# Two causal convolutions moved behind other products, a softplus cut in two, and one subtraction given to another engine, in a hybrid decoder layer

## The chip, the core and the metric

The kernel runs on one core of a Trainium2 chip. A core has a matrix engine (PE, whose weight loads are shown apart as PEld) and three engines for elementwise work: VectorE (DVE), ScalarE (ACT) and GpSimd (POOL). SyncE (SP) issues the DMA transfers. Each engine works through its own instructions in the order in which they were written, and semaphores make one engine wait for another. The metric is the time of one execution on the device in microseconds; the kernel before took 1659.45 us (median of 3 runs).

## The reference

One decoder layer over 1040 positions (16 learned positions ahead of 1024 tokens), width 1024, float32. The stage that the change touches is the first: normalised rows times the columns of `w_in`, and what hangs directly on them.

```python
xn = rms_norm(h, mix_pre_g)
proj = xn @ w_in                       # z | x,B,C | dt | q | k | v
xbc = silu(causal_dwconv(xbc, conv_w, conv_b))   # 4 taps a channel, then x, B and C
dt = softplus(dt_raw + dt_bias)
A = -exp(a_log)                        # decays come from cumulative sums of dt * A
...                                    # SSD mixer, stick-breaking attention, w_out, gated FFN
```

A causal depthwise convolution with four taps is, for each channel (a partition) and all 1040 positions, one multiply-add with the bias and three more multiply-adds.

## The kernel before

**Precision.** Every matrix product is made of three: each operand is split into a high part (rounded, written by ACT as a copy) and a low part (the operand minus its high part, by POOL or DVE), and high x high, low x high and high x low are summed. So each block of weights costs ACT a copy and POOL or DVE a subtraction before PE can use it. Names that end in `hi`/`h` are high parts, `lo`/`l` low ones: `whi4z` and `wlo4z` are the two parts of one block of z's weights.

**Products in pairs.** Two blocks of 128 output columns are made together by a scheme of seven half-size products (class `Duo`, `product`, lines 260 to 321) in place of eight. The order in which they are issued is 1, 6, 5, 7, 2, 3, 4, for the first pair (`i == 0`) 1, 5, 2, 6, 7, 3, 4. Each is 24 matmuls of 260 columns into one of three PSUM accumulators, which the trace calls `dA`, `dX` and `dY` followed by the pair's name (`dXx`, `dXz`). Products 6, 7 and 4 go into X one after another: each adds to what is there, and between them DVE (line 320, `craw_x<-dXx,...`) adds the accumulator's present value into the pair's rows `craw`. So the first matmul of the next product into the same accumulator waits for that DVE sum. Products 5 and 3 share Y in the same way, 1 and 2 share A, which ACT copies out (line 317).

**The pairs.** x00 (first two blocks of x), z00, x02, z02, then B/C of the second group, and so on. Weights of the following pair are prepared while one is multiplied: `split_22` (lines 273 to 279: ACT line 277, POOL line 278) for the block `a22`, `sums` (POOL, lines 281 to 288) for four sums of weights, `split_3`, `split_1`, `split_4` (ACT line 181, POOL line 182). For pair z00 these are `ahz`/`alz`, `wrz`/`s24z`, `whi3z`/`wlo3z`, `whi1z`/`wlo1z`, `whi4z`/`wlo4z`. Low parts of the activations' own sums (`t2l`, `t3l`, `t4l`, line 255) are made by DVE.

**Work hung into slots.** B and C of the first group were projected before the pairs. Their four taps (`tap`, lines 502 to 509: DVE, one TENSOR_SCALAR at line 505 and three SCALAR_TENSOR_TENSOR at line 508), the SiLU (ACT, line 512) and for B the turning by PE into token order (`to_tokens`, tiles `tt_B_0` to `tt_B_2`, evacuated by ACT at lines 492 and 497 into `xtkB`) are hung behind the seven products: `slots[j]` is issued after the j-th product of a pair, slot 7 after the first of the next. The same lists hold the parts of dt (`dt_acts`, line 625): `loads` (`fold`), `turn_dt` (18 small matmuls into `tpd`, line 649), the softplus (`soft_a`, `soft_b`: an exponential by ACT, then a series on DVE with tiles of 128x144) and the decays (`pz`).

**Orders and buffers that matter here.** PE, DVE, ACT and POOL keep the written order; SP's transfers are ordered by a planner. `tt_B_0`, `tt_B_1`, `tt_B_2` and `tpd` are taken in this order from one pool of two PSUM buffers: `tpd` gets the buffer of `tt_B_1`, and so waits until ACT has emptied that one.

Of the kernel before, what the change touches and what calls it, by code (L numbers as in the profile page):

```python
# [9 lines left out]
F32 = mybir.dt.float32  # L10
# [3 lines left out]
ALU = mybir.AluOpType  # L14
# [52 lines left out]
def tile_layer(ctx: ExitStack, tc: tile.TileContext, x, meta, rows, parts,  # L67
               w_z, w_xbc, w_dt, w_q, w_k, w_v, w_out, w_up, w_down, out):
    nc = tc.nc
# [15 lines left out]
    def psum_mm(name):  # L85
        return ps[0].tile([P, 512], F32, tag="mm", name=name, bufs=ps[1])
# [86 lines left out]
    def weight_rows(flat, n, o):  # L173
        return flat[:, o:o + n * WR].rearrange("p (k c) -> p k c", c=WR)[:, :, :P]
# [77 lines left out]
    def split_t(raw, hl, eng):  # L252
        h, l = hl
        nc.scalar.activation(h, raw, AF.Copy)
        eng.tensor_tensor(l, raw, h.bitcast(F32), op=ALU.subtract)
        return hl

    class Duo:
# [11 lines left out]
        def split_1(self):  # L270
            self.w["a11"], self.w["a12"] = split_w(self.r[0], f"1{self.nm}")

        def split_22(self):
            h, l = (weight_rows(sa.tile([P, 5 * P], F32R, tag=f"a22{e}", name=f"a{e}{self.nm}", bufs=2), 4, OFF22)
                    for e in "hl")
            raw = self.r[1][:, HI4]
            nc.scalar.activation(h, raw, AF.Copy)
            nc.gpsimd.tensor_tensor(l, raw, h.bitcast(F32), op=ALU.subtract)
            self.w["a22"] = h, l

        def sums(self):
# [217 lines left out]
    def conv_acts(b, raw, nm, turned, store):  # L499
        box = {}  # L500

        def tap(j):
            if j == 0:
                box["d"] = sa.tile([P, L], F32, tag="cd", name=f"cd{nm}", bufs=2)
                nc.vector.tensor_scalar(box["d"], raw[:, 0:L], conv_w[:, b, 0:1], conv_b[:, b:b + 1],
                                        op0=ALU.mult, op1=ALU.add)
            else:
                nc.vector.scalar_tensor_tensor(box["d"], raw[:, j:j + L], conv_w[:, b, j:j + 1], box["d"],
                                               op0=ALU.mult, op1=ALU.add)

        def silu():
            nc.scalar.activation(box["d"], box["d"], AF.Silu)
            if store is not None:
                nc.sync.dma_start(out=store, in_=box["d"])

        def skip():
            xd = raw[:, 0:L]
            nc.scalar.activation(xd, box["d"], AF.Copy, scale=ssd_d[:, b:b + 1])
            nc.sync.dma_start(out=xdd[b // 4][b % 4], in_=xd)

        def turn_(part):
            if part == 0:
                box["t"] = s3.tile([P, NT + 1, P], F32, tag="xtk", name=f"xtk{nm}", bufs=2)
            to_tokens(box["d"], box["t"], nm, part)
            if part == 2:
                turned(box["t"])

        taps_ = [lambda j=j: tap(j) for j in range(4)] + [silu] + [skip] * (b < 8)
        return taps_, [lambda k=k: turn_(k) for k in range(3)] if turned else []
# [16 lines left out]
    def store_bn(g):  # L546
        def store(t):
            nc.sync.dma_start(out=bnd[g][:NM, 0], in_=t[:NM, 0])
            nc.sync.dma_start(out=bnd[g][:, 1:], in_=t[:, 1:])
        return store  # L550
# [58 lines left out]
    b0_taps, b0_turns = conv_acts(8, chains[0][0], "B0", store_bn(0), bcd[0][0])  # L609
# [15 lines left out]
    def dt_acts():  # L625
        box = {}

        def t3(name):
            return s3.tile([P, NT + 1, 16], F32, name=name, tag=name)
# [26 lines left out]
        def soft_a():  # L656
            dtx = box["dtx"]
            e, s, s2 = box["e"], box["s"], box["s2"] = [t3(n) for n in ("e1", "s1", "s2")]
            nc.vector.scalar_tensor_tensor(e, dtx, -1.0, dtx, op0=ALU.mult, op1=ALU.min)
            nc.scalar.activation(e, e, AF.Exp)  # L660
            nc.vector.tensor_scalar(s, e, 2.0, None, op0=ALU.add)
            nc.vector.reciprocal(s, s)
            nc.vector.tensor_tensor(s, s, e, op=ALU.mult)
            nc.vector.tensor_tensor(s2, s, s, op=ALU.mult)
# [13 lines left out]
        def decay(k):  # L678
            lhs = (tri, low, ones)[k]
            pz, adt, dst = psum_mm(f"pz{k}"), box["s2"], dtk[:, 2 + k]  # L680
            w0 = P if k == 2 else NM
            mm(pz[:w0, 0:16], lhs[:NM, :w0], adt[:NM, 0, :], start=True, stop=True)
            mm(pz[:, 16:NA], lhs, adt[:, 1:, :], start=True, stop=True)
            nc.scalar.activation(dst[:w0, 0, :], pz[:w0, 0:16], AF.Exp)
            nc.scalar.activation(dst[:, 1:, :], pz[:, 16:NA].rearrange("p (a b) -> p a b", b=16), AF.Exp)
            if k == 0:
                nc.vector.tensor_copy(dtk[:NM, 1, 0, :], pz[:NM, 0:16])
                nc.vector.tensor_copy(dtk[:, 1, 1:, :], pz[:, 16:NA].rearrange("p (a b) -> p a b", b=16))
# [15 lines left out]
        def store():  # L704
            nc.sync.dma_start(out=dtkd, in_=dtk)

        return [[loads], [turn_dt], [soft_a], [soft_b], [lambda: decay(0)], [lambda: decay(1)],
                [lambda: decay(2), store, turn_acs]]

    v_stack = ExitStack()  # L710
# [2 lines left out]
    def fetch_v(kh, fh, pool, name="q", key=None):  # L713
        tiles = []
        for s in range(2):
            if pool is None:
                tiles.append(wp.tile([P, 2, 512], F32, tag="wraw", name=f"v{name}{kh}{fh}{s}"))
            else:
                tiles.append(pool.tile([P, 2, 512], F32, tag=f"v{kh}{fh}{s}", name=f"v{name}{kh}{fh}{s}"))
            r0 = (4 * kh + 2 * s) * P  # L720
            nc.sync.dma_start(out=tiles[s], in_=w_v[r0:r0 + 2 * P, 512 * fh:512 * fh + 512].rearrange(
                "(b p) c -> p b c", p=P))
        vq[key or (kh, fh)] = tiles
# [9 lines left out]
    def v_split(n, s):  # L733
        raw = vq[VRAW[VSPEC[n][0]]][s]
        h, l = (wp.tile([P, 2, 512], F32R, tag=f"w{e}", name=f"vw{e}{n}{s}", bufs=WB) for e in ("hi", "lo"))
        nc.scalar.activation(h, raw, AF.Copy)
        nc.vector.tensor_tensor(l, raw, h.bitcast(F32), op=ALU.subtract)
        vops[n, s] = h, l

    def merged(*lists):  # L740
        return [sum(parts_, []) for parts_ in zip(*lists)]

    c0_taps, _ = conv_acts(10, chains[1][0], "C0", None, bcd[0][1])
    dts = dt_acts()
    slots = [b0_taps[:2] + dts[0], b0_taps[2:4], b0_taps[4:], [], c0_taps[:2] + b0_turns[:1],
             c0_taps[2:4] + b0_turns[1:2], c0_taps[4:] + b0_turns[2:], dts[1]]
    for i, q in enumerate(duos):
        n = duos[i + 1] if i + 1 < len(duos) else None
        if i + 2 < len(duos):
            duos[i + 2].load()  # L750
        for j, m in enumerate((1, 5, 2, 6, 7, 3, 4) if i == 0 else (1, 6, 5, 7, 2, 3, 4)):
            q.product(m)
            if i == 0:
                if m == 1:
                    d0.split_4()
                elif m == 6:
                    split_t(t4l.bitcast(F32), xo["t4"], nc.vector)
            if n is not None:
                if m == 1:
                    n.split_22()  # L760
                elif m == 6:
                    n.sums()
                elif m == 7:
                    n.split_3()
                elif m == 2:
                    n.split_1()
                elif m == 3:
                    n.split_4()
            elif m in (7, 2):
                v_split(1, int(m == 2))  # L770
            for act in slots[j]:
                act()
        extra = slots[7:]
        slots = q.done(q)
        for k, acts_ in enumerate(extra):
            slots[k] = acts_ + slots[k]
        if i == 1:
            slots = merged(slots, [[], dts[2], [], dts[3], [], [], []]) + [dts[4], dts[5], dts[6]]
        if i == n_early:
            t_stack.close()  # L780
            vl = v_stack.enter_context(tc.tile_pool(name="vl", bufs=1, side="left"))
            fetch_v(1, 0, vl)
        if i + 2 == len(duos):
            fetch_v(0, 0, None)
# [887 lines left out]
    op = opool.enter_context(tc.tile_pool(name="outp", bufs=2, side="right"))  # L1672
# [574 lines left out]
    for i in range(2, NFF):  # L2247
        q = probs[i]
        n = probs[i + 1] if i + 1 < NFF else None
# [73 lines left out]
    slots = [ta.tile([P, 4 * HW], F32, tag=f"{n}{e}", name=f"slot{n}{e}") for n in ("b22", "t4") for e in "hl"]  # L2323
# [48 lines left out]
    for s in range(n2):  # L2372
        n, a, b, p = steps2[s]
# [122 lines left out]
```

## Time and profile before

| what | us |
|---|---|
| median of 3 runs (1658.9 to 1659.69) | 1659.45 |
| the profiled execution | 1663.12 |
| its span, first to last instruction | 1661.4 |
| PE busy in it | 1627.9 |
| DVE, ACT, POOL busy | 1091.1, 747.7, 780.6 |

The stage of the first projections with its pairs runs from the span's start to about 330 us. In rows of a timeline the columns are start, duration, engine, line, operation, out<-in and shape, and in brackets the engine's idle time before it and what ended that. PE's matmuls overlap: 24 of them start 0.12 us apart, so that a product takes 2.88 us. Between 162 and 330 us PE is busy all the time; between 50 and 162 it has a few short waits, which the prediction shows.

### The profile page before, as it was taken

How to read it: one execution, taken by the hardware profiler on the slowest of the kernel's cores; microseconds unless marked ns; L12 is line 12 of the kernel's file. 1: busy time of each engine (PE TensorE's matmuls, PEld its weight loads, DVE VectorE, ACT ScalarE, POOL GpSimd, SP SyncE). 2: the span in 40 equal slices, each digit the busy share in tenths (PEclk: the TensorE clock that was granted, in tenths of full speed). 3: DMA queues.
4: the chain of work that ended last, by engine and by line, in shares of the span. 5: the costliest groups of instructions: out<-in, count | busy, mean ns of one | idle time of the engine just before them, and what ended most of it. 6: DMA issues, size and time to landing. Idle time of an engine off the chain costs nothing.

```text
span 1661.4 us, 28993 instructions
## 1 busy us (share of the span) xinstructions
PE 1627.9 (98%) x11508; PEld 1433.2 (86%) x11508; DVE 1091.1 (66%) x1248; ACT 747.7 (45%) x1100; POOL 780.6 (47%) x579
## 2 busy tenths in 40 slices
PE   7999999999999999999999999999999999999998
PEld 6999999978777788888877889999999999888886
DVE  7975744344367689999840677766566655658877
ACT  7444344332234367767652435433333333344544
POOL 2876877520357463455431113777777767200001
PEclk9999999999999999999999999999999999999999
DMA  4543235334577776545254542232233332495335
GB/s 175 184 152 132 102 120 195 134 136 146 144 223 237 248 224 198 153 142 152 68 178 148 176 165 90 96 96 95 95 98 109 114 106 83 140 331 175 95 116 182
DMA packets 164518, 247.39 MB, mean 149 GB/s; under 512 B 18487, under 2 KB 99495, under 8 KB 162702
## 3 DMA queue, kind: packets, MB, share of 16 engines
q1 hardware_dynamic: 163806, 244.48, 45.8%
q8 instruction: 91, 1.49, 0.4%
q10 hardware_dynamic: 576, 1.05, 0.2%
q14 instruction: 45, 0.37, 0.1%
HBM read 161.99 MB, written 83.46 MB: 148 GB/s over the span
## 4 chain that ended last, share of the span: by engine, by line
PE 86%; DVE 4%; DMA 3%; POOL 3%; issue 2%; SPq 1%; ACT 1%; POOLq 0%; DVEq 0%; ACTq 0%
PE fX L1900 10%; PE mo L1504 10%; PE dnA L2312 7%; PE fY L1900 7%; PE fA L1900 7%; PE dnB L2312 5%; PE av L1352 3%; PE tw L1332 3%; PE z L1308 3%; DVE kp L1314 2%; PE dXz L308 2%; PE dXqk L308 2%; PE vA L819 2%; PE pj_q L218 2%; PE pj_k L218 2%
## 5 line engine op out<-in xcount | busy, mean ns | idle before, releaser
L1314 DVE TENSOR_TENSOR_SCAN kp<-kp,hold 128x396 f32<-128x396 f32 (+5 forms) x224 | 211.1, 1013 | 20.2 <-ACT kp L1309 18.3
L182 POOL TENSOR_TENSOR wlo<-wr,whi 128x1024 fp32r<-128x1024 f32 x43 | 99.3, 2318 | 41.0 <-ACT whi L181 41.0
L2349 POOL TENSOR_TENSOR fms<-fms 128x1 f32<-128x1 f32 x8 | 2.3, 287 | 222.0 <-DMA ar<-fda 185.9
L181 ACT ACTIVATE whi<-wr 128x1024 fp32r<-128x1024 f32 x43 | 45.7, 1063 | 112.2 <-PE fX L1900 73.5
L1972 DVE SCALAR_TENSOR_TENSOR ga<-gr,pp,ga 128x1024 f32<-128x1024 f32 x44 | 69.3, 1575 | 34.0 <-ACT ga L1965 33.2
L2234 ACT ACTIVATE dh<-ar 128x512 fp32r<-128x512 f32 x77 | 48.6, 631 | 94.7 <-PE dnB L2312 44.7
L2235 DVE TENSOR_TENSOR dl<-ar,dh 128x512 fp32r<-128x512 f32 x77 | 53.2, 691 | 47.1 <-ACT dh L2234 47.1
L1309 ACT ACTIVATE kp<-z 128x788 f32<-128x788 f32 (+4 forms) x96 | 72.7, 832 | 16.6 <-PE z L1308 12.2
L1337 ACT ACTIVATE th<-tw 128x1024 f32<-128x1024 f32 (+2 forms) x96 | 70.8, 813 | 15.6 <-PE tw L1332 15.6
L1352 PE MATMUL av<-th,v 128*64 128x128 f32 x1152 | 70.0, 275 | 2.0 <-POOL tmsa L985 0.9
L1332 PE MATMUL tw<-ident,kp 128*128 128x128 f32 x576 | 70.0, 276 | 0.8 <-DVE kp L1314 0.4
L1352 PEld LDWEIGHTS av<-th,v 128*64 128x64 f32 x1152 | 62.3, 137 | 8.1 <-issue 3.9
L1332 PEld LDWEIGHTS tw<-ident,kp 128*128 128x128 f32 x576 | 62.4, 141 | 8.0 <-issue 7.0
L2312 PE MATMUL dnA<-dl,dh 128*128 128x512 f32 x176 | 68.5, 389 | 0.0
L2312 PE MATMUL dnA<-dh 128*128 128x512 f32 x176 | 68.5, 389 | 0.0
L2312 PE MATMUL dnA<-dh,dl 128*128 128x512 f32 x176 | 68.5, 389 | 0.0
L1286 POOL TENSOR_SCALAR cb<-kp 128x32 f32<-128x32 f32 x64 | 42.9, 678 | 50.6 <-DVE kp L1314 44.3
L2033 POOL TENSOR_TENSOR al<-wr,ah 128x512 fp32r<-128x512 f32 x20 | 28.6, 1431 | 77.5 <-ACT ah L2032 77.4
L1308 PE MATMUL z<-k,q 64*128 64x396 f32 (+9 forms) x672 | 62.3, 329 | 1.0 <-DVE st L941 1.0
L1308 PEld LDWEIGHTS z<-k,q 64*128 64x128 f32 x672 | 53.1, 185 | 10.7 <-ACT th L1337 4.2
L2312 PE MATMUL dnB<-dh 128*128 128x512 f32 x132 | 51.3, 389 | 0.0
L2312 PE MATMUL dnB<-dh,dl 128*128 128x512 f32 x132 | 51.3, 389 | 0.0
(987 smaller groups left out, 6027.2 us busy)
## 6 DMA issues: line engine op xcount, KB each, us to landing
wr<-in_w_up SPq DMA_DIRECT2D x44, 512.0 KB
fds<-ga SPq DMA_DIRECT2D x44, 256.0 KB
b<-in_w_down SPq DMA_DIRECT2D x44, 256.0 KB
ar<-fds SPq DMA_DIRECT2D x44, 256.0 KB
fda<-ga SPq DMA_DIRECT2D x33, 256.0 KB
ar<-fda SPq DMA_DIRECT2D x33, 256.0 KB
k<-qkd SPq DMA_DIRECT2D x8, 1040.0 KB
q<-qkd SPq DMA_DIRECT2D x64, 128.0 KB
```

What stands on the lines that cost most here:

```text
L182: nc.gpsimd.tensor_tensor(l, raw, h.bitcast(F32), op=ALU.subtract)
L218: mm(acc[:, :CQ - s], a[:, k, :], b[:, k % 4, c + s:c + CQ], start=(k == 0 and j == 0), stop=(k == KB - 1 and j == 2))
L1308: mm(z[:, j, a - lo:e - lo], u[h, :], r[h, a - bases[x]:e - bases[x]], start=s_ == 0, stop=s_ == 2)
L1309: nc.scalar.activation(kp[:, :, lo:top], z[:, :, :top - lo], AF.Sigmoid, scale=-QSCALE)
L1314: nc.vector.tensor_tensor_scan(part, part, hold[:, L - last + a:L - last + e][:, ::-1], 1.0 if e == last else kp[:, j, e:e + 1], op0=ALU.m ...
L1332: nc.tensor.transpose(tw[:, j, b, :], kp[:, j, c0:c0 + P], ident)
L1337: copied[0] = nc.scalar.activation(th[:, :, :nb, :], tw[:, :, :nb, :], AF.Copy, scale=-1.0, bias=1.0).ins
L1352: mm(av[halves[j], 1 - x, :], v[:, kb, halves[j]], th[:, j, b, :], start=kb == 0, stop=kb == i)
L1504: recent[0] = mm(acc, u[:, k, :], v[:, cs], start=(k == 0 and j == 0), stop=(k == 7 and j == 2))
L1900: mm(acc[:, c, :nn], u[:, k, :], v[:, k, c0:c0 + nn], start=first and k == 0 and j == 0, stop=k == 3 and j == 2, skip_group_check=not first)
L1972: nc.vector.scalar_tensor_tensor(v, self.g[jj][:, :, i:i + 256], fconv_w[:, j, i:i + 1], v, op0=ALU.mult, op1=ALU.add)
L2312: mm(banks[BANK[n], t], u[:, 0, c], v[:, 1, :], start=(n in (1, 2, 5) and p == 0 and i == 0), stop=(p == NPR - 1 and i == 2), skip_group_c ...
```

## The change

Three edits, all in the first stage. First, `slots` of pair x00: B's first two taps move from behind its first product to behind its second, B's other taps and C's taps follow one place later each or are regrouped, and the turning of B goes with them. Second, `soft_a` ends after the exponential; the four DVE instructions that followed it become `soft_m`, hung one product later. Third, the low part of z00's block `a22` (`alz`, line 278) is made by DVE in place of POOL; later pairs keep POOL.

```diff
-        def split_22(self):
+        def split_22(self, eng=nc.gpsimd):
...
             nc.scalar.activation(h, raw, AF.Copy)
-            nc.gpsimd.tensor_tensor(l, raw, h.bitcast(F32), op=ALU.subtract)
+            eng.tensor_tensor(l, raw, h.bitcast(F32), op=ALU.subtract)
...
             nc.vector.scalar_tensor_tensor(e, dtx, -1.0, dtx, op0=ALU.mult, op1=ALU.min)
             nc.scalar.activation(e, e, AF.Exp)
+
+        def soft_m():
+            e, s, s2 = box["e"], box["s"], box["s2"]
             nc.vector.tensor_scalar(s, e, 2.0, None, op0=ALU.add)
             nc.vector.reciprocal(s, s)
             nc.vector.tensor_tensor(s, s, e, op=ALU.mult)
...
-        return [[loads], [turn_dt], [soft_a], [soft_b], [lambda: decay(0)], [lambda: decay(1)],
+        return [[loads], [turn_dt], [soft_a], [soft_m], [soft_b], [lambda: decay(0)], [lambda: decay(1)],
                 [lambda: decay(2), store, turn_acs]]
...
-    slots = [b0_taps[:2] + dts[0], b0_taps[2:4], b0_taps[4:], [], c0_taps[:2] + b0_turns[:1],
-             c0_taps[2:4] + b0_turns[1:2], c0_taps[4:] + b0_turns[2:], dts[1]]
+    slots = [dts[0], b0_taps[:2], b0_taps[2:3], b0_taps[3:], c0_taps[:1], c0_taps[1:3] + b0_turns[:1],
+             c0_taps[3:] + b0_turns[1:2], b0_turns[2:] + dts[1]]
...
-                    n.split_22()
+                    n.split_22(nc.gpsimd if i else nc.vector)
...
-            slots = merged(slots, [[], dts[2], [], dts[3], [], [], []]) + [dts[4], dts[5], dts[6]]
+            slots = merged(slots, [[], dts[2], dts[3], [], dts[4], [], []]) + [dts[5], dts[6], dts[7]]
```

DVE during the first pair, from the low part of t3 (`t3l`) to the sum of product 6 (`craw_x_840<-dXx`), before:

```order
L505 TENSOR_SCALAR cdB_851<-craw_B_256,pp 128x1040
L508 SCALAR_TENSOR_TENSOR cdB_851<-craw_B_256,pp,cdB_851 128x1040
L636 TENSOR_TENSOR fold<-ident 32x16
L255 TENSOR_TENSOR t3l<-t3r,t3h 128x2080
L320 TENSOR_TENSOR craw_x_838<-dYx_867,craw_x_838 128x520
L508 SCALAR_TENSOR_TENSOR cdB_851<-craw_B_256,pp,cdB_851 128x1040 x2
L320 TENSOR_TENSOR craw_x_840<-dXx_926,craw_x_838 128x520
```

The same stretch of DVE, and on to the sum of product 7, with the change:

```order
L255 TENSOR_TENSOR t3l<-t3r,t3h 128x2080
L278 TENSOR_TENSOR alz_848<-wrz_802,ahz_847 128x4x128
L636 TENSOR_TENSOR fold<-ident 32x16
L320 TENSOR_TENSOR craw_x_838<-dYx_864,craw_x_838 128x520
L505 TENSOR_SCALAR cdB_890<-craw_B_256,pp 128x1040
L508 SCALAR_TENSOR_TENSOR cdB_890<-craw_B_256,pp,cdB_890 128x1040 x2
L320 TENSOR_TENSOR craw_x_840<-dXx_923,craw_x_838 128x520
L255 TENSOR_TENSOR t4l<-t4l,t4h 128x2080
L508 SCALAR_TENSOR_TENSOR cdB_890<-craw_B_256,pp,cdB_890 128x1040
L320 TENSOR_TENSOR craw_x_838<-dXx_923,craw_x_838 128x520
```

B's first two taps stood ahead of `t3l` and now stand between the sums of products 5 and 6, where `alz` was added too; one tap left that place for one behind `t4l`.

ACT at the end of the first pair: the evacuations of B's three turned tiles (`xtkB<-tt_B_0`, `_1`, `_2`) and the SiLU of C (`cdC<-cdC`), before:

```order
L492 ACTIVATE xtkB_991<-tt_B_0_992 16x128
L181 ACTIVATE whi4z_1020<-s24z_954 128x8x128
L497 ACTIVATE xtkB_991<-tt_B_1_1026 128x512
L512 ACTIVATE cdC_988<-cdC_988 128x1040
L497 ACTIVATE xtkB_991<-tt_B_2_1059 128x512
```

And with the change:

```order
L181 ACTIVATE whi4z_1015<-s24z_951 128x8x128
L492 ACTIVATE xtkB_1021<-tt_B_0_1022 16x128
L512 ACTIVATE cdC_988<-cdC_988 128x1040
L497 ACTIVATE xtkB_1021<-tt_B_1_1053 128x512
L317 ACTIVATE craw_z_1088<-dAz_1063 128x520
```

The evacuation of `tt_B_1` stood ahead of C's SiLU and now stands behind it. PE's own rows there keep their order (`tt_B_2`, then `tpd`, then product 6 of z00), only the turnings of B lie one product later among them.

DVE in the third pair, between the sums of products 6, 5 and 7 (tile `e` is the softplus's exponential, `s` what follows from it), before:

```order
L659 SCALAR_TENSOR_TENSOR e_1403<-dtx 128x144
L661 TENSOR_SCALAR s_1404<-e_1403 128x144
L662 RECIPROCAL s_1404<-s_1404 128x144
L663 TENSOR_TENSOR s_1404<-s_1404,e_1403 128x144
L664 TENSOR_TENSOR s_1405<-s_1404 128x144
L320 TENSOR_TENSOR craw_x_1349<-dYx_1412,craw_x_1349 128x520
```

And with the change:

```order
L659 SCALAR_TENSOR_TENSOR e_1403<-dtx 128x144
L320 TENSOR_TENSOR craw_x_1349<-dYx_1408,craw_x_1349 128x520
L664 TENSOR_SCALAR s_1404<-e_1403 128x144
L665 RECIPROCAL s_1404<-s_1404 128x144
L666 TENSOR_TENSOR s_1404<-s_1404,e_1403 128x144
L667 TENSOR_TENSOR s_1405<-s_1404 128x144
```

The sum of product 5 moved ahead of the four instructions on `s`.

## The prediction

> **What bounds the kernel now.** I read the page's busy times first, then the waits of PE in the stage that the change touches, then that stage in slices, then the chain of work, then the timelines of DVE, POOL and ACT.
>
> ```profile
> span 1661.4 us, 28993 instructions
> PE 1627.9 (98%) x11508; PEld 1433.2 (86%) x11508; DVE 1091.1 (66%) x1248; ACT 747.7 (45%) x1100; POOL 780.6 (47%) x579
> 162.00:330.00 168.00, 168.00 (x1406) 167.91 (x1405) 80.11 (x71) 64.97 (x87) 118.29 (x62) 1.00 0.40 141
> PE dYx L308 <- DVE craw_x L320: 1.3, 1, 1.3
> PE dXz L308 <- POOL wlo4z L182: 1.0, 1, 1.0
> PE dXx L308 <- DVE craw_x L320: 1.0, 1, 1.0
> PE dAx L308 <- ACT craw_x L317: 0.7, 1, 0.7
> PE dXx L308 <- POOL wlo4x L182: 0.3, 1, 0.3
> ```
>
> PE is the bound, and from 162 to 330 us it is busy without a break (168.00 of 168.00): what PE loses or gains before 162 arrives there whole. Between 50 and 165 us it waits five times (the five rows), 4.3 us in all. A second loss shows in the granted clock and in the chain:
>
> ```profile
> 67.75:71.16 3.41, 2.48 (x20) 2.49 (x21) 1.05 (x3) 2.90 (x2) 3.41 (x2) 1.00 0.82 318
> 81.40:84.81 3.41, 2.54 (x21) 2.26 (x20) 3.32 (x6) 1.90 (x3) 3.41 (x2) 1.00 0.49 167
> 84.82:88.22 3.40, 3.25 (x15) 3.25 (x16) 2.98 (x2) 0.66 (x2) 2.69 (x3) 0.50 0.78 312
> 84.97 4.35 PE dXz L308 x22
> 89.32 2.88 PE dYz L308 x24
> L649 PE MATMUL tpd<-fold,sq 32*128 32x16 f32 (+1 forms) x18 | 2.1, 250 | 0.0
> ```
>
> From 84.82 to 88.22 us the clock (third number from the end) is 0.50, and the product that runs then takes 4.35 us where the next takes 2.88: 1.47 us lost behind a wait of 1.0. The slice ahead held that wait and the 18 small matmuls of `tpd`, and lost the clock; the slice from 67.75, with a wait of 0.96, kept it.
>
> **How DVE and POOL share.** These rows carry the sum:
>
> ```profile
> 58.24 0.81 DVE L505 TENSOR_SCALAR cdB<-craw_B,pp 128x1040 f32<-128x1040 f32 x1
> 59.09 1.30 DVE L508 SCALAR_TENSOR_TENSOR cdB<-craw_B,pp,cdB 128x1040 f32<-128x1040 f32 x1
> 60.30 0.15 DVE L636 TENSOR_TENSOR fold<-ident 32x16 f32<-32x16 f32 x1
> 60.39 2.31 DVE L255 TENSOR_TENSOR t3l<-t3r,t3h 128x2080 fp32r<-128x2080 f32 x1
> 62.62 0.68 DVE L320 TENSOR_TENSOR craw_x<-dYx,craw_x 128x520 f32<-128x520 f32 x1
> 63.23 2.62 DVE L508 SCALAR_TENSOR_TENSOR cdB<-craw_B,pp,cdB 128x1040 f32<-128x1040 f32 x1
> 65.89 2.12 DVE L508 SCALAR_TENSOR_TENSOR cdB<-craw_B,pp,cdB 128x1040 f32<-128x1040 f32 x1
> 67.93 0.69 DVE L320 TENSOR_TENSOR craw_x<-dXx,craw_x 128x520 f32<-128x520 f32 x1
> 62.09 2.67 POOL L182 TENSOR_TENSOR wlo4x<-s24x,whi4x 128x1024 fp32r<-128x1024 f32 x1 [5.96 <-ACT whi4x L181]
> 64.71 2.20 POOL L278 TENSOR_TENSOR alz<-wrz,ahz 128x512 fp32r<-128x512 f32 x1
> 67.52 2.55 POOL L182 TENSOR_TENSOR wlo1z<-wrz,whi1z 128x1024 fp32r<-128x1024 f32 x1
> 68.67 0.39 PE L308 MATMUL dXx<-t3h,whi3x 128*128 128x260 f32 x1 [0.96 <-DVE craw_x L320]
> ```
>
> A tap takes 1.30 alone (59.09) but 2.62 at 63.23: POOL's `wlo4x` runs until 64.76, and the tap ends 1.09 after that. POOL's `alz` then ends at 66.91, 1.06 after the tap's end at 65.85; the next tap ends 1.10 after `alz`. The two take turns, whole instructions at a time; the one that waited pays 0.2 less than its free time. The sums out of PSUM (line 320) keep their 0.68 beside a running POOL. A half-size instruction of POOL costs 1.06 in its turn, a full one 2.06 (`wlo1z`: ends 70.07, the tap before it 68.01).
>
> **The change, part one: what stands ahead of product 6's sum.** PE's product 7 waits for DVE's sum at 67.93 (last row above). Before, DVE had done B's first two taps in the hole between `t2l` and `t3l`, while ACT made `t3h`. That hole stays, empty: `t3h` waits for `t2l` as it did.
>
> ```profile
> 58.35 1.95 ACT L254 ACTIVATE t3h<-t3r 128x2080 fp32r<-128x2080 f32 x1 [3.37 <-DVE t2l L255]
> 64.79 1.05 ACT L181 ACTIVATE whi1z<-wrz 128x1024 fp32r<-128x1024 f32 x1
> 48.29 0.68 DVE L407 TENSOR_TENSOR t4r<-t4r,t2r 128x512 f32<-128x512 f32 x1
> ```
>
> `t3l` ends at 62.70 as before. `alz` on DVE, free price 0.68 as for `t4r` of the same 512 elements, waits its turn behind `wlo4x` (64.76): 65.23. `fold` and the sum of product 5 (0.15, 0.68, each starting 0.08 before the last ends): 65.92. B's first tap starts at 65.84, 0.08 before POOL can start `wlo1z` (`whi1z` ends 65.84, and POOL started 0.08 after ACT at 62.09): 66.65. `wlo1z` 68.71, second tap 69.80, POOL's first sum of weights 70.86, third tap 71.95, sum of product 6 72.56. PE starts product 7 at 72.6 in place of 68.67: **+3.9**. If `wlo1z` wins the near tie, the first tap waits for it: 1.1 more. Without any turn of POOL after `wlo4x` the same list ends near 69.7 (+1.1); so the bounds are +1.1 and +5.0, and I take 3.9, since all rows above show turns.
>
> PE then idles from 67.7 to 72.6, through the whole slice 67.75 to 71.16. If that halves the clock in the next slice (to 74.57), PE loses half of 2.0 us: **+1.0**, bounds 0 and 1.7 (half a slice).
>
> **Part two: the second wait.**
>
> ```profile
> 81.41 0.18 PE L649 MATMUL tpd<-fold,sq 32*16 32x16 f32 x1
> 79.62 0.58 ACT L497 ACTIVATE xtkB<-tt_B 128x512 f32<-128x512 f32 x1
> 82.91 1.07 ACT L512 ACTIVATE cdC<-cdC 128x1040 f32<-128x1040 f32 x1 [2.71 <-DVE cdC L508]
> 118.33 2.19 POOL L182 TENSOR_TENSOR wlo3z<-wrz,whi3z 128x1024 fp32r<-128x1024 f32 x1
> ```
>
> From 68.67 to `tpd` at 81.41 PE needed 12.7 us without a wait; the same work stands there now, so PE reaches `tpd` at 72.6 + 12.7 + 1.0 = 86.3. But `tpd` takes the PSUM buffer of `tt_B_1`, whose evacuation (before at 79.62, ahead of the SiLU at 82.91) now stands behind C's SiLU on ACT. The SiLU needs C's fourth tap, so DVE's turns decide. From 71.95, with the prices above: POOL's second sum of weights 73.0; `t4l` (2.31 less 0.2) 75.1; third sum 76.2; B's fourth tap 77.3; fourth sum 78.3; C's first tap 78.9. ACT does B's SiLU and `whi3z` (1.07, 1.05) by 79.45, then `wlo3z` (2.19 alone, the row at 118.33) 81.7; C's second tap 82.8; `wlo4z` 84.9; third tap 86.0; sum of product 4 86.6; fourth tap, alone, 87.8; SiLU 88.95; evacuation 89.45. PE waits from 86.3 to 89.5: **+3.2**. `tpd` takes its 2.0, and product 6 of z00 starts at 91.5. Its slice (88.23 to 91.64) holds a wait and `tpd`, as the one from 81.40 did, so I take 0.50 until 95.05: 3.4 us at half clock lose 1.7, and the product ends at 91.5 + 2.9 + 1.7 = 96.1. Before, it ended at 89.32. **Difference +6.8**, in which the old wait for `wlo4z` and its 1.47 are already gone (`wlo4z` is ready by 84.9, under the new wait).
>
> [...]
>
> **Part three: the softplus.**
>
> ```profile
> 118.50 2.18 DVE L664 TENSOR_TENSOR s<-s 128x144 f32<-128x144 f32 x1
> 120.60 0.69 DVE L320 TENSOR_TENSOR craw_x<-dYx,craw_x 128x520 f32<-128x520 f32 x1
> 78.64 0.33 SPq L268 DMA_DIRECT2D wrz<-in_w_z  x1
> ```
>
> `s<-s` waits its turn behind the `wlo3z` of 118.33, and the sum of product 5, behind it on DVE, keeps product 3 waiting 1.3. With the sum ahead of those four that wait goes: **-1.3**. What is late instead is the sum of product 7, which product 4 needs one product (2.9 us) later: nothing. Splitting costs no instruction; giving `alz` to DVE takes 1.2 off POOL, which has slack in either case. SP issues the same transfers; z02's first weights now stand ahead of B's store, and the load still waits for the fourth sum of weights (78.64 before, 78.3 now).
>
> **The sum.** 6.8 - 1.3 = +5.5 us on the profiled execution (span 1661.4, whole 1663.12). That lies 3.7 above the median of the runs; I carry the difference over: 1659.45 + 5.5 = **1665.0**. Its own range: no half clocks (-2.7), or tie lost and a longer half clock (+1.1 and +1.7): 1662.3 to 1667.8.
>
> **Rivals.** (a) *The waits go and none comes*: DVE reaches product 6's sum in time, since its list there is only some 4.5 us long without POOL's turns. Then 1.03 + 1.47 + 1.3 = 3.8 are saved: 1655.7. Against it: every pair of overlapping rows shows turns, and the hole before `t3l` is wasted. 12%. (b) *Only the first wait comes*: if DVE and ACT gain 3 us before C's SiLU, `tpd` runs at 86.3 and z00's product 6 ends at 86.3 + 2.0 + 2.9 = 91.2, 1.9 after 89.32; less 1.3, that is +0.6: 1660.1. For it: the list behind 72.6 is long and each price small. Against it: most of it is POOL's own work, which nothing shortens. 14%. (c) *`tpd` at half clock*: its 18 matmuls take 2.0 more, with the tie lost as well: 1668.1. 4%. My forecast: 70%.
>
> **Numbers.** A measurement of this kernel tells 0.2%, 3.3 us, from no change. The forecast is slower by more in nearly all of its range (67 of 70), with (c) 71%; (b) and the forecast's lower end make 16% for within; (a), and the lucky end of (b), 13% for faster. The range 1658.3 to 1668.5 leaves out (a) and the tails.
>
> **What would show it.** Right: PE's wait for `craw_x` L320 before product 7 of about 5 us; a new wait of `tpd` for ACT `xtkB`, 2 to 4 us; no wait of `dXz` for `wlo4z` and none of product 3 of x02; slices at 0.50 after one or both. Wrong: product 7 still starting near 68.7, DVE instructions of 1.30 beside a busy POOL, or a `tpd` that does not wait.

## The result, and the profile after

The changed kernel takes 1669.28 us (median of 6 runs, 1668.04 to 1670.66) beside 1659.72 for the kernel before (6 runs, 1658.9 to 1662.85). The ratio is 1.0053, with a 95% interval of 1.0042 to 1.0064: 7.0 to 10.6 us slower. The prediction had the sign right and said 1665.0, with 1668.5 as the upper end of its range; the time lies 4.3 above the one and 0.8 above the other.

The profiled execution took 1668.39 us. Its page, and the waits of PE from 40 to 175 us (total, times, longest):

```profile
span 1666.7 us, 28993 instructions
PE 1631.9 (98%) x11508; PEld 1438.5 (86%) x11508; DVE 1087.6 (65%) x1249; ACT 748.1 (45%) x1100; POOL 775.0 (47%) x578
```

```profile
PE dXx L308 <- DVE craw_x L320: 5.0, 1, 5.0
PE tpd L649 <- ACT xtkB L497: 2.3, 1, 2.3
PE dAx L308 <- ACT craw_x L317: 0.6, 1, 0.6
PE dXx L308 <- POOL wlo4x L182: 0.3, 1, 0.3
```

The wait of product 7 for DVE's sum has grown from 1.0 to 5.0 us, and `tpd` waits for ACT's `xtkB`. The wait for `wlo4z` (1.0) and that of product 3 of x02 (1.3) are gone. The first products started 0.98 us earlier in this execution (first matmul into `dAx` at 53.56, before at 54.54), so 0.98 is added to a time of this timeline before it is compared with one of before. The rows that decide, from the timelines of DVE, POOL, ACT and PE:

```profile
64.87 0.80 DVE L505 TENSOR_SCALAR cdB<-craw_B,pp 128x1040 f32<-128x1040 f32 x1
65.70 5.33 DVE L508 SCALAR_TENSOR_TENSOR cdB<-craw_B,pp,cdB 128x1040 f32<-128x1040 f32 x2
70.96 0.69 DVE L320 TENSOR_TENSOR craw_x<-dXx,craw_x 128x520 f32<-128x520 f32 x1
...
64.93 2.80 POOL L182 TENSOR_TENSOR wlo1z<-wrz,whi1z 128x1024 fp32r<-128x1024 f32 x1 [0.59 <-ACT whi1z L181]
67.68 2.27 POOL L285 TENSOR_TENSOR wrz<-wrz 128x512 f32<-128x512 f32 x1
...
87.04 1.07 ACT L512 ACTIVATE cdC<-cdC 128x1040 f32<-128x1040 f32 x1 [6.24 <-DVE dtx L651]
88.02 0.58 ACT L497 ACTIVATE xtkB<-tt_B 128x512 f32<-128x512 f32 x1
...
71.70 0.58 PE L308 MATMUL dXx<-t3h,whi3x 128*128 128x260 f32 x1 [5.04 <-DVE craw_x L320]
...
88.65 0.42 PE L649 MATMUL tpd<-fold,sq 32*16 32x16 f32 x3 [2.31 <-ACT xtkB L497]
...
91.63 0.59 PE L308 MATMUL dXz<-t2h,whi4z 128*128 128x260 f32 x1
```

B's two further taps take 5.33 us together instead of 2.6 (twice the 1.30 of a tap alone, before), since `wlo1z` (2.80) and a sum of weights (2.27) get their turns between them. C's SiLU comes at 87.04, and only behind it is the buffer for `tpd` emptied. The same stretch by slices (PE busy, PEld, DVE, ACT, POOL, then the granted clock):

```profile
65.66:69.07 3.41, 1.00 (x9) 0.79 (x7) 3.34 (x3) 2.52 (x2) 3.41 (x2) 1.00 0.98 378
69.07:72.48 3.41, 0.78 (x3) 0.78 (x4) 3.41 (x3) 0.70 (x1) 3.33 (x3) 0.50 0.02 9
72.49:75.90 3.41, 3.41 (x18) 3.41 (x17) 3.41 (x2) 0.00 (x0) 3.33 (x2) 0.50 0.00 0
...
86.14:89.55 3.41, 1.10 (x11) 0.87 (x9) 0.89 (x2) 2.51 (x5) 0.00 (x0) 1.00 0.18 74
89.55:92.96 3.41, 3.41 (x17) 3.37 (x17) 1.18 (x4) 0.54 (x2) 3.12 (x3) 0.50 0.58 236
92.97:96.38 3.41, 3.41 (x18) 3.41 (x18) 2.10 (x1) 0.00 (x0) 3.33 (x3) 0.50 0.00 0
```

Behind each wait the clock is 0.50 for two slices, not for one. Product 7 takes 4.86 us (71.70 to 76.56), `tpd` 2.98, product 6 of z00 5.11 (to 96.74).

### The profile page after: what moved, and what is told of

Read it like the earlier page. It is cut to its first block, busy times and chain, and to the rows that moved or that the text cites. A ratio compares the mean times of both kernels' runs of the same rounds, so it can differ in the third digit from the quotient of the medians.

```text
span 1666.7 us, 28993 instructions
## 1 busy us (share of the span) xinstructions
PE 1631.9 (98%) x11508; PEld 1438.5 (86%) x11508; DVE 1087.6 (65%) x1249; ACT 748.1 (45%) x1100; POOL 775.0 (47%) x578
## 3 DMA queue, kind: packets, MB, share of 16 engines
q8 instruction: 91, 1.49, 0.4%
## 4 chain that ended last, share of the span: by engine, by line
PE 87%; DVE 3%; issue 2%; DMA 1%; SPq 1%; POOL 1%; ACT 0%; DVEq 0%; POOLq 0%; ACTq 0%
PE fX L1903 10%; PE mo L1507 10%; PE dnA L2315 7%; PE fY L1903 7%; PE fA L1903 7%; PE dnB L2315 5%; PE av L1355 4%; PE tw L1335 3%; PE z L1311 3%; PE dXz L308 2%; PE dXqk L308 2%; PE pj_q L218 2%; PE pj_k L218 2%; DVE kp L1317 2%; PE vB L822 2%
```

## The experiments

Theory 1 is the prediction's: the longer list ahead of product 6's sum, worked off in turns with POOL; then `xtkB` behind C's SiLU; and a half clock after each wait. The rivals: one edit alone does all of it (`alz` on DVE); the second wait is hidden anyway; half clocks are what costs, or they cost nothing. A further question is the base: the sum was made against one execution, 3.7 us above the median.

All runs are put on one scale here, since the later stages scatter from execution to execution (from the fourth pair to the end the profiles need 1507.2 to 1513.6 us, in no order that follows the edits). The kernels b_again, a_again and e1_soft to e9_both were measured on one chip, e10_tpd2 to e12_warm on a second and e13_late on a third, each beside the kernel before; between these groups only the ratios are compared. The columns are the time of each kernel's profile from the first matmul of product 1 of x00 to the first matmul of product 7 of x00, of `tpd`, of product 5 of z00 (where product 6 ends), and of product 1 of the fourth pair; and the median of the timed runs with its ratio to the kernel before, measured beside it.

| kernel | product 7 | tpd | product 5 of z00 | fourth pair | median us | ratio, 95% interval |
|---|---|---|---|---|---|---|
| before, first profile | 14.14 | 26.88 | 34.62 | 95.82 | 1659.72 | |
| before, second (b_again) | 14.12 | 26.83 | 34.54 | 94.19 | 1661.85 | 0.9999, 0.9990 to 1.0007 |
| changed, first profile | 18.14 | 35.08 | 43.17 | 102.82 | 1669.28 | 1.0053, 1.0042 to 1.0064 |
| changed, second (a_again) | 18.14 | 35.06 | 41.58 | 101.23 | 1669.22 | 1.0051, 1.0037 to 1.0064 |
| e1_soft | 14.15 | 26.87 | 35.37 | 95.55 | 1661.06 | 0.9997, 0.9987 to 1.0008 |
| e2_slots | 17.34 | 34.99 | 43.09 | 102.73 | 1669.88 | 1.0053, 1.0040 to 1.0065 |
| e3_alz | 20.51 | 34.66 | 41.18 | 100.83 | 1667.85 | 1.0041, 1.0028 to 1.0055 |
| e4_turn | 18.14 | 33.33 | 38.33 | 97.98 | 1665.20 | 1.0022, 1.0013 to 1.0032 |
| e7_hole | 13.94 | 32.16 | 40.28 | 99.95 | 1665.59 | 1.0032, 1.0020 to 1.0044 |
| e9_both | 13.95 | 28.31 | 33.31 | 92.95 | 1660.83 | 0.9996, 0.9987 to 1.0005 |
| e10_tpd2 | 13.95 | 28.31 | 36.67 | 96.50 | 1664.40 | 1.0015, 1.0006 to 1.0024 |
| e11_split | 13.95 | 28.29 | 33.49 | 96.11 | 1661.08 | 0.9998, 0.9989 to 1.0007 |
| e12_warm | 18.20 | 31.10 | 37.62 | 97.26 | 1662.10 | 1.0010, 1.0001 to 1.0019 |
| e13_late | 13.93 | 27.93 | 32.93 | 96.39 | 1662.28 | 1.0004, 0.9995 to 1.0013 |

### Both kernels again

> The kernel before, unchanged, profiled again. The profiled execution of before that the sum stood on took 1663.12 us, 3.7 above the median of its runs. If that execution was an ordinary one, this one shows the same waits and half clocks of PE (slices at 0.50 from 84.8 and from 470.5 us) and a span near 1661.4. If it was a slow one, the span is near 1658 and some of its waits or half-clock slices are gone: then the sum was made against the wrong base. In either case the ratio to the kernel before is 1.000.

> The changed kernel, unchanged, profiled and timed again beside the kernel before. If the loss is what its first profile shows against the second profile of before (8.6 us from the first product of the pairs to the first of the fourth pair), the ratio is 1.0045 to 1.006. If the forecast's base was sound and its sum right, 1.0025 to 1.0035. The profile shows the wait of product 7 of x00 near 5.0 us, that of tpd 2 to 3 us, and slices at 0.50 behind both.

Measured beside the kernel before again, the change gives 1.0051; the loss is real and not a matter of the first six runs. Its profile shows the two waits, 5.0 us for product 7 and 1.8 for `tpd`, a little under the 2 to 3 expected. The medians of the kernel before in the later comparisons, 15 to 27 runs each, are 1661.1 to 1661.7, about 2 us above the 1659.45 that the prediction started from. The second profile of before has a span of 1660.1 us, between the two that were expected, and the slice at 0.50 from 470.5 us isn't in it. Its waits of PE from 40 to 175 us:

```profile
PE dXz L308 <- POOL wlo4z L182: 1.0, 1, 1.0
PE dXx L308 <- DVE craw_x L320: 1.0, 1, 1.0
...
```

The wait of 1.3 us for the sum of product 5 ahead of product 3 of x02, which the prediction saved with the softplus, isn't there. From product 5 of z00 to the fourth pair this profile needs 59.65 us, as the changed kernel does (59.65 in both of its profiles); the first profile of before needs 61.20.

The rows show what decides about that wait. In the second profile of before:

```profile
110.58 0.20 ACT L229 ACTIVATE craw_x<-ones 128x3 f32<-128x3 f32 x1 [3.33 <-DMA xdd<-craw_x]
118.63 0.31 DVE L664 TENSOR_TENSOR s<-s 128x144 f32<-128x144 f32 x1
119.08 2.20 POOL L182 TENSOR_TENSOR wlo3z<-wrz,whi3z 128x1024 fp32r<-128x1024 f32 x1 [0.65 <-ACT whi3z L181]
```

And ACT's row in the first:

```profile
110.46 0.20 ACT L229 ACTIVATE craw_x<-ones 128x3 f32<-128x3 f32 x1 [4.04 <-DMA xdd<-craw_x]
```

It is a near tie. On the table's scale `s<-s` starts at 63.25 in the second profile, ahead of `wlo3z` (63.70), and takes 0.31 us; in the first it comes at 63.96, behind `wlo3z` (63.79), and takes 2.18. DVE's series was 0.7 us later in the first profile because ACT, whose exponential stands ahead of it, had waited 0.7 us longer for a DMA transfer and then worked without a break.

In the second profile of the changed kernel the clock behind `tpd` was 0.50 for one slice (91.74 to 95.15) and not two, and product 6 of z00 ended 1.6 us sooner, at 41.58. So the same program loses 7.0 or 8.6 us up to there (41.58 or 43.17, less 34.6).

### The parts alone

In e1_soft only the softplus is cut in two:

```diff
...
-        return [[loads], [turn_dt], [soft_a], [soft_b], [lambda: decay(0)], [lambda: decay(1)],
+        return [[loads], [turn_dt], [soft_a], [soft_m], [soft_b], [lambda: decay(0)], [lambda: decay(1)],
...
```

> The kernel before with the softplus split alone. All theories: PE's wait of 1.3 us for the sum of product 5 ahead of product 3 of x02 is gone and nothing takes its place, all other waits as in the kernel before: about -1.3 us, ratio 0.9992, between 0.998 and 1.000.

There is no wait of product 3 of x02 in its profile, and nothing in its place; the time can't be told from the kernel before. The interval (2.2 us less to 1.3 more) can't tell the expected -1.3 from nothing either. Two other kernels with the whole softplus (e2_slots, e3_alz) have no such wait: there, too, `s<-s` came ahead of `wlo3z`. So the wait stands in one of four profiles with the whole softplus, and its removal is worth 1.3 us only in executions in which the tie is lost; how many those are, no run here tells.

In e2_slots only the list of slots is the new one, in e3_alz only `alz` is given to DVE:

```diff
...
-                    n.split_22()
+                    n.split_22(nc.gpsimd if i else nc.vector)
```

> The kernel before with the new places of B's and C's taps and turnings alone; alz stays on POOL, the softplus whole. Theory 1 (the list ahead of product 6's sum in turns with POOL, xtkB behind C's SiLU, half clock after each): product 7 waits 3 to 4.5 us, tpd 2.5 to 3.5 us, slices at 0.50 behind both; +7 to +9 us, ratio 1.0042 to 1.0054. Rival (what costs is alz on DVE, which empties the hole ahead of t3l): the first wait stays near 1 us, about +2 us, ratio 1.001.

> The kernel before with alz of z00 on DVE alone; taps keep their old places in the text, and the softplus is whole. In the written order of this kernel B's first two taps stand behind t3l and alz, since alz is written ahead of them, needs ACT's ahz and comes behind t3l. Theory 1: four taps then stand ahead of product 6's sum, product 7 waits 6 to 7.5 us with slices at 0.50 behind it; tpd waits for nothing new and dXz of z00 not for wlo4z; about +5 to +7 us, ratio 1.003 to 1.0042. Rival (the move of the taps is the cause, alz on DVE is free): product 7's wait stays near 1 us, ratio 0.999 to 1.000.

PE's two longest waits in e2_slots, and the longest in e3_alz:

```profile
PE dXx L308 <- DVE craw_x L320: 3.6, 1, 3.6
PE tpd L649 <- ACT xtkB L497: 3.4, 1, 3.4
...
```

```profile
PE dXx L308 <- DVE craw_x L320: 7.4, 1, 7.4
...
```

Theory 1 holds in both, with its numbers: 3.6 and 3.4 where 3 to 4.5 and 2.5 to 3.5 were expected, 7.4 where 6 to 7.5 was. The rival of each falls. But they are no terms of a sum: 1.0053 and 1.0041 alone, 1.0051 together, because each of them empties the hole ahead of `t3l` by itself. In e3_alz no one moved the taps. `alz` was written ahead of them, it needs ACT's `ahz`, and DVE did both taps only behind `t3l` and `alz` (65.87 and 66.72; `t3l` 61.03, `alz` 63.27); four taps then stood ahead of product 6's sum. In the text of the kernel before, too, `t3l` (line 606) is written ahead of the taps, and yet DVE did the two taps first: here the order that reached the engine is not that of the text. What moved the taps ahead is not on record; the runs show that it did so where no `alz` stood between (before, e7_hole), and not in e3_alz.

Two slices of e3_alz around `tpd` (which runs from 89.92 to 91.94):

```profile
89.21:92.62 3.41, 3.41 (x30) 3.22 (x29) 1.45 (x6) 2.57 (x4) 0.49 (x1) 1.00 0.37 151
92.62:96.03 3.41, 3.41 (x18) 3.41 (x17) 3.37 (x2) 0.00 (x0) 3.25 (x3) 0.50 0.40 159
```

PE is busy for all 3.41 us of the first, without a wait, and the clock is still halved in the next. The prediction had put the half clock of the kernel before down to the wait of 1.0 and `tpd` together; here the 2.02 us of `tpd` alone did it.

### One wait mended, then both

e4_turn takes the second wait away, e7_hole the first, e9_both both. In e4_turn B's second turning is hung ahead of C's last tap and SiLU:

```diff
-             c0_taps[3:] + b0_turns[1:2], b0_turns[2:] + dts[1]]
+             b0_turns[1:2] + c0_taps[3:], b0_turns[2:] + dts[1]]
```

In e7_hole B's first two taps stand in slot 0 again, and `alz` is written behind them:

```diff
                 if m == 1:
-                    n.split_22(nc.gpsimd if i else nc.vector)
+                    if i:
+                        n.split_22()
...
             for act in slots[j]:
                 act()
+            if i == 0 and m == 1:
+                n.split_22(nc.vector)
...
-    slots = [dts[0], b0_taps[:2], b0_taps[2:3], ...
+    slots = [b0_taps[:2] + dts[0], [], b0_taps[2:3], ...
```

The expectations of e4_turn, e7_hole and e9_both, in this order:

> The changed kernel with B's second turning hung ahead of C's fourth tap and SiLU, so that ACT empties the buffer for tpd first. Theory 1: tpd waits no more and runs at full clock (2.0 us); product 7's wait of 5 us and its half clock stay; product 6 of z00 still loses about 1.5 us behind tpd. 3.5 to 5 us less than the changed kernel: ratio to before 1.002 to 1.0035. Rival (the second wait is hidden anyway, wlo4z or C's taps are as late): a wait of 2 to 3 us for wlo4z takes its place, ratio 1.0045 or more.

> The changed kernel with B's first two taps written back behind product 1 and alz (still on DVE) written behind them, so that both taps stand ahead of t3l again; all else as in the change. Theory 1: product 7 does not wait, no slice at 0.50 near 70 us; tpd, now reached near 81, waits 2 to 3 us for xtkB, with one or two slices at 0.50 behind it: ratio 1.0005 to 1.002. Rival (DVE's share of POOL's work is itself too much): product 7 still waits over 1 us, ratio 1.003 or more.

> The hole filled as in the run before, and B's second turning ahead of C's SiLU as well; the softplus is split, alz is on DVE. Theory 1: no wait of product 7 and none of tpd; dXz of z00 waits about 1.5 us for wlo4z; one slice at 0.50 behind tpd. Ratio 0.9985 to 1.0005. If tpd's small matmuls alone, without a wait of more than 1 us, do not halve the clock, that slice is gone and the ratio is at the lower end.

Against the second median of the changed kernel (1669.22) these give -4.0, -3.6 and -8.4 us: within the noise the two add up, and together they are the whole loss. In e4_turn the wait of product 7 is the same 5.0, `tpd` doesn't wait, and nothing took the place of its wait; the 1.5 us that product 6 of z00 was still to lose behind `tpd` didn't come (2.98 us from its first matmul to the next product's). In e7_hole product 7 waits 0.8, but the ratio, 1.0032, is over the expected 1.002; its waits of PE, and then the chain of work (start, duration, what):

```profile
PE tpd L649 <- ACT xtkB L497: 3.8, 1, 3.8
PE tt_B L491 <- ACT cdB L512: 1.5, 1, 1.5
PE dXx L308 <- DVE craw_x L320: 0.8, 1, 0.8
...
```

```profile
85.54 3.66 PE tpd L649 x18
89.20 4.62 PE dXz L308 x24
```

The wait of `tpd` came out as 3.8 instead of 2 to 3: longer than a slice (3.41). `tpd` itself then took 3.66 us in place of 2.0, as at half clock, and product 6 lost 1.7 behind it (4.62 against 2.88). And B's first turning waits 1.5 us for B's SiLU, a wait that I had not foreseen: with the taps early PE reaches the turning sooner, but B's last tap still stands behind `t4l` on DVE.

The chain of e9_both in the same place:

```profile
82.94 2.02 PE tpd L649 x18
84.96 3.07 PE dXz L308 x24
```

`tpd` isn't waiting, and product 6 runs at full clock; the expected wait for `wlo4z` and the slice at 0.50 didn't come. Up to product 5 of z00 this kernel is 1.3 us ahead of before (33.31 against 34.6). Its time, 0.9996 of before, can't be told from no change.

### The clock by itself

In the profiles of the eight kernels so far, in the stretch from 50 to 165 us and from full clock, the next slice was at 0.50 where PE's waits in a slice and the time of `tpd`'s small matmuls together filled 2.02 us or more of its 3.41 (over half), and at 1.00 where they filled 1.49 or less. Three kernels test what would follow if that went on. e10_tpd2 is e9_both with `tpd`'s matmuls made twice:

```diff
-            for i in range(NT + 1):
+            for i in 2 * list(range(NT + 1)):
```

> The kernel with both waits mended (hole filled, B's second turning ahead of C's SiLU), but tpd's small matmuls made twice, with the same results: about 2 us more of them, next to no wait beside them. The profiles so far say that the clock of a slice of 3.41 us is 0.50 when PE spent over about half of the slice ahead in waits or in tpd's matmuls (2.02 us and more: halved; 1.49 and less: kept). Theory half-slice: 4 us of small matmuls put over 2 us into at least one slice, whatever its phase, so one or two slices at 0.50 follow, without any wait: +2.0 for the matmuls (up to 2 more if they themselves run at half clock) and +1.5 to +3 for the half clock: ratio to before 1.001 to 1.003. Rival (only whole idle slices halve the clock, and small matmuls are work): no slice at 0.50 there, +2.0 alone, ratio about 1.0008.

The chain of work, and three slices:

```profile
82.85 4.04 PE tpd L649 x36
86.90 4.45 PE dXz L308 x24
```

```profile
81.32:84.73 3.41, 3.41 (x32) 3.21 (x30) 3.41 (x3) 0.00 (x0) 2.59 (x1) 1.00 0.74 283
84.73:88.14 3.41, 3.41 (x31) 3.32 (x31) 1.51 (x5) 2.57 (x4) 0.94 (x1) 1.00 0.35 145
88.14:91.55 3.41, 3.41 (x18) 3.41 (x17) 3.11 (x3) 0.00 (x0) 3.25 (x3) 0.50 0.44 170
```

The first slice holds 1.88 us of `tpd` (82.85 to 84.73), and the next keeps its clock; that one holds 2.17 (to 86.90), and 0.50 follows, with PE busy throughout. Up to product 5 of z00 the kernel needs 3.4 us more than e9_both (36.67 against 33.31): 2.0 for the matmuls and 1.4 for product 6 at half clock (4.45 against 3.07). By the ratios it is 3.2 us (1.0015 against 0.9996, with intervals that don't touch). The rival (small matmuls are work, and only an idle slice halves the clock) falls.

e12_warm is e4_turn with 36 matmuls, whose result nothing uses, between products 6 and 7 of x00:

```diff
+        def warm(self):
+            (hi, lo), (xh_, xl_) = self.w["a22"], xo["b11"]
+            for c in (0, 1, 0):
+                for k in range(4):
+                    for u, v in ((hi, xh_), (hi, xl_), (lo, xh_)):
+                        mm(self.acc["A"][:, c, :CQ], u[:, k, :], v[:, k, c * CQ:(c + 1) * CQ], start=True, stop=True)
...
+            if i == 0 and m == 7:
+                q.warm()
```

> The kernel with only the second wait mended (product 7 still waits 5 us), with 36 further matmuls of 260 columns into an accumulator that nothing reads any more, written between product 6 and product 7, so that PE works through 4.3 of the 5 us (their results are used by nothing). Theory half-slice: product 7 still starts when DVE's sum is there (a wait of 0.3 to 0.9 us is left), but no slice at 0.50 follows and product 7 takes 2.9 to 3.0 us in place of 4.9: about -2 us against the kernel without them, ratio to before 1.0005 to 1.0017. Rival (the half clock costs little, the waits are all; or the matmuls hold up DVE): product 7 is no earlier done, ratio 1.002 or more.

```profile
67.43 4.33 PE dAx L327 x36
...
71.79 0.70 DVE craw_x L320
...
72.53 3.17 PE dXx L308 x24
...
85.50 2.02 PE tpd L656 x18
87.52 4.59 PE dXz L308 x24
```

Product 7 starts when it did (18.20 against 18.14), but takes 3.0 us (72.53 to 75.53) in place of e4_turn's 5.4 (72.80 to 78.17), and PE reaches `tpd` 2.2 us sooner (31.10 against 33.33). So the half clock behind the wait of 5.0 us cost 2.0 to 2.5 us (4.86 in the first profile of the changed kernel, 5.37 in e4_turn, in place of 2.88), and 36 useless matmuls inside the wait saved them here. By the ratios the kernel is 2.0 us faster than e4_turn (1.0010 against 1.0022), but the two intervals overlap, so it is the profile that shows the saving. The last two rows show why the profile gives only 0.7 of it at product 5 of z00: here the 2.02 us of `tpd` (85.50 to 87.52) fell whole into the slice from 84.14 to 87.56, and product 6 ran at half clock; in e4_turn 1.43 us of it fell into one slice, and the clock stayed.

### Towards a faster kernel

e11_split is e9_both with `tpd` cut in two (10 matmuls behind product 1 of z00, 8 behind product 6) and C's taps a product later; e13_late leaves `tpd` whole, with C's taps and B's first turning later. The slots of e13_late against those of e9_both:

```diff
-    slots = [b0_taps[:2] + dts[0], [], b0_taps[2:3], b0_taps[3:], c0_taps[:1], c0_taps[1:3] + b0_turns[:1],
-             b0_turns[1:2] + c0_taps[3:], b0_turns[2:] + dts[1]]
+    slots = [b0_taps[:2] + dts[0], [], b0_taps[2:3], b0_taps[3:], [], c0_taps[:2],
+             b0_turns[:2] + c0_taps[2:3], b0_turns[2:] + dts[1] + c0_taps[3:]]
```

> The kernel with both waits mended, tpd's small matmuls cut in two (10 behind product 1 of z00, 8 behind product 6), and C's taps one product later, so that POOL's wlo4z has fewer turns of DVE ahead of it. Theory half-slice: no slice at 0.50 between 55 and 160 us in any execution; waits of PE under 1 us each, 3 us in all against 4 us and a half-clock loss of 1.5 in the kernel before: 2 to 3 us less than before, ratio 0.998 to 0.999. Rival (waits saved here come back in the later stages, as the small gain of the kernel with both waits mended may say): ratio 0.9995 to 1.0005.

> The kernel with both waits mended, and besides C's taps and B's first turning one product later (tpd whole), so that the first turning waits less for B's SiLU. Theory: the wait of 1.5 us of the first turning is gone, dXz of z00 waits 0.5 to 1 us for wlo4z, product 7 as before 0.8; one slice at 0.50 behind tpd or none, by its phase. From the first product of the pairs to the start of product 5 of z00 32 to 34.5 us against 34.6 in the kernel before: 1 to 2 us less, ratio 0.9987 to 0.9997. Rival (as where tpd was cut: work moved later costs as much behind z00): no difference, with a new wait of over 0.5 us between 100 and 160 us.

Neither beats the kernel before. Both are ahead at product 5 of z00 (33.49 and 32.93 against 34.6), with no slice at 0.50 between 55 and 160 us (in e13_late the two around `tpd`, from 80.90 to 87.72, are at 1.00), and both lose it again before the fourth pair. Waits of e11_split, then of e13_late:

```profile
...
PE pz L689 <- DVE s L682: 1.0, 1, 1.0
...
PE dAx L308 <- POOL wlo1x L182: 0.7, 1, 0.7
```

```profile
PE pz L685 <- DVE s L678: 1.1, 1, 1.1
PE dXx L308 <- issue: 1.1, 1, 1.1
...
PE dAx L308 <- POOL wlo1x L182: 0.6, 1, 0.6
...
PE dXz L308 <- DVE craw_z L320: 0.5, 1, 0.5
```

From product 5 of z00 to the fourth pair they need 3.0 and 3.8 us more than e9_both, of which these waits (without the `issue` row) are 1.7 and 2.2. The likely reason, which no run isolates: what DVE does later for C and for `tpd`, it does later for x00's taps, for the softplus and in turns with POOL too, so that `pz` and x02's first product wait. In e13_late the wait of the first turning is gone as expected, but the row with `issue`, 1.1 us, came in its place: product 4 of x00 starts at 75.41, 0.1 us after DVE ended the sum of product 7, which stood behind B's fourth tap there. The rival expected for each is what happened. The best of the kernels here is e9_both, level with the kernel before.

## Why the prediction was half right

**The first wait: right.** Product 7 was to start at 72.6; it started at 71.70, or 72.68 with the 0.98 added. Each price in turns held: the sum of product 6 was to end at 72.56, and ended at 72.63 (70.96 + 0.69 + 0.98). The near tie went as assumed, the first tap (64.87) ahead of `wlo1z` (64.93). The turns are there again: two taps beside `wlo1z` and a sum of weights took 5.33 us, where two taps alone take 2.6. What makes the two engines take turns, no run here shows.

**The half clock behind it: half its size, without effect.** One slice and +1.0 were forecast; it was two slices and +2.0 (product 7 took 4.86), in the second profile +2.5 (5.33). PE reached `tpd` 1.0 or 1.5 later than forecast, and waited 2.3 or 1.8 there instead of 3.2: the second wait absorbed the error, which is luck.

**The second wait: right.** `tpd` was to be released at 89.5; it started at 89.63 in the first profile (88.65 + 0.98), and at 89.60 in the second on the same scale (35.06 + 54.54). The mechanism was shown by e4_turn, which moves that turning with its evacuation alone.

**What follows `tpd`: right in one profile, 1.6 short in the other.** Product 6 of z00 was to end at 96.1. On the same scale it ended at 96.12 (41.58 + 54.54) in the second profile, and at 97.7 in the first, where `tpd` itself ran at half clock (2.98 in place of 2.0) and 0.50 lasted a second slice. The forecast knew one slice only; where the slices fall on the program differed between these two executions (the first at 0.50 behind `tpd` starts 35.99 us after the first matmul of product 1 of x00 in the first profile, 37.07 in the second). The average of the two is +7.8 where the sum had +6.8.

**The softplus: the term that failed.** -1.3 was taken from a wait that one execution of the kernel before showed, as if it were always there. It hangs on a near tie between DVE and POOL, and in the second profile of before the tie went the other way; e2_slots and e3_alz, with the whole softplus, don't have the wait either. Against such executions the term is 0. That e1_soft gives 0.9997 agrees, but its interval would allow -1.3 too.

**The base: the other step that failed.** The difference was carried over to 1659.45, the median of three runs, as if the profiled execution had been 3.7 us slow. The later medians are 1661.1 to 1661.7 (84 runs), and by them that execution, 1663.12, was 1.4 to 2 us above the ordinary time. Part of that is the lost tie: its wait belonged to this execution and was subtracted from a base that didn't hold it.

In sum: +7.8 and no gain from the softplus, in place of 6.8 - 1.3, make up 2.3 of the 4.3 us that were missing. The remaining 2 are the base, which is argued and not shown: the six runs of before that stand beside the changed kernel have a median of 1659.72, 9.6 us below it, and only the second comparison gives 7.7 (1669.22 against 1661.5). 7.8 us lies inside the interval of both (7.0 to 10.6, and 6.1 to 10.6). Between the two first profiles the difference is 5.3 us (1668.39 against 1663.12), close to the forecast 5.5, and that is luck: up to product 5 of z00 it is 8.6 and not 6.8, the lost tie of before takes off 1.6, and 1.7 more go outside the stretch (0.98 ahead of the pairs, 0.7 behind the start of the fourth). What stays open is the scatter of the later stages, in which nothing here shows an effect of the change.

**The rivals.** (a) (no wait) and (b) (only the first) are refuted by the wait rows. (c) (`tpd` at half clock) is what happened in one of two profiles, though without the lost tie; its 4% were far too few.

## What to carry to other kernels

The order of an engine's work can change through an instruction that waits, not only through one that is moved: putting a dependent subtraction (`alz`) on DVE pushed two taps out of a hole that had cost nothing (in e3_alz they started at 65.87 and 66.72, and product 7 waited 7.4 us), while with the same subtraction written behind the taps the hole was filled again and no loss is left to see (e9_both). A wait of one execution is no term of a sum before a second profile shows it, least of all where its rows are a near tie. And behind the wait of 5.0 us another 2.0 to 2.5 us were lost at a clock of 0.50: independent matmuls inside the wait (36 useless ones in e12_warm) saved those in the profile (product 7 in 3.0 us against 5.4), though it is better to have no wait.

## What the runs showed that I had not expected

In these profiles the granted clock changes by slices of 3.41 us, which lie differently on the program in the two executions of the changed kernel (35.99 and 37.07 us, above), and it is not idleness alone that counts. In the stretch from 50 to 165 us, from full clock, a slice was followed by 0.50 where PE's waits and the 32x16 matmuls of `tpd` together filled 2.02 us of it or more (2.02 in e3_alz and e12_warm, 2.17 in e10_tpd2, 2.41 of waits alone in the changed kernel from 65.66 us), and never where they filled 1.93 or less (1.93 in e13_late, 1.88 in e10_tpd2, 1.49 of waits alone in e9_both). If one limit parts them, my estimate from these profiles is that it lies between 1.93 and 2.02, hardly more apart than the modelled ends of matmuls allow to tell (the chain of the changed kernel has product 6 of z00 start at 91.70, its timeline at 91.63). From 0.50 the clock stayed there for another slice after a much smaller gap (1.2 us of waiting in e4_turn from 71.59 us). So the same 2.02 us of `tpd` cost 1.5 us in e12_warm (product 6 in 4.59) and nothing in e9_both (3.07), by where the slices fell.

In other stages it went otherwise. In the changed kernel the slice from 454.78 us was followed by 0.50 with 1.66 us of waits in it (PE busy for 1.75 of 3.41), and one without any wait was too (PE, PEld, DVE, ACT, POOL, then the granted clock):

```profile
598.14:601.55 3.41, 3.41 (x31) 3.23 (x31) 3.41 (x3) 0.99 (x2) 3.33 (x3) 1.00 0.97 327
601.55:604.96 3.41, 3.41 (x24) 2.94 (x24) 1.79 (x4) 1.17 (x4) 2.94 (x5) 0.50 0.97 280
```

Matmuls of other kinds run there (in the first slice shown 18 with one column, `pta`, take 2.1 us); how they count, no run here tells.

Half clock came after a slice in which PE issued matmuls throughout (3.41 of 3.41 in e3_alz) as after one with 2.41 us of waits (the changed kernel). Whether it is the few rows, the few columns or the time between the matmuls of `tpd` that counts, no run here tells.
